# Fixed start addresses for the operands of the weight products in a one-layer HGRN2 + ConvFFN kernel

## The chip, the cores and the metric

The kernel runs on one core of a Trainium2 chip. Its time is the device time of one execution in microseconds (us). The median of three executions before the change is 1764.19 us (1764.08 to 1764.83).

## The reference

One layer of a hybrid backbone with `D_MODEL` 2048 works on 256 latent tokens `x` and 256 context tokens `ctx`, all in float32. Cut to what matters here:

```python
mods = silu(c) @ ada_w + ada_b                     # 2048 x 12288, shift/scale/gate rows
h_l, h_c = modulate(rms_norm(x) ...), modulate(rms_norm(ctx) ...)
q, f_fw, f_bw, v, g = split(h @ hgrn_w_in, 5)      # 2048 x 10240
o = bidirectional gated scan over q, f, v          # 16 heads of 128
y = (rms_norm(o) * silu(g)) @ hgrn_w_out           # 2048 x 2048
x1 = x + gate * rms_norm(y)
gate, up = split(modulate(rms_norm(x1) ...) @ ffn_w_in, 2)   # 2048 x 11264
out = x1 + gate2 * rms_norm((silu(conv3(gate)) * up) @ ffn_w_out)   # 5632 x 2048
```

Nearly all arithmetic is in the four products with `hgrn_w_in`, `hgrn_w_out`, `ffn_w_in` and `ffn_w_out`. Context tokens go through `hgrn_w_in` only.

## The kernel before

Every float32 operand of a weight product is split in two float32r parts, a high part (ScalarE's cast, L95) and the rest (VectorE's subtraction, L96). One product then becomes three matmuls, issued by `mm3`: high by high (L192), high by low (L193), low by high (L194). Below they are called the first, second and third matmul of a triple.

The weights come as a stream of 456 tiles (`Stream`), each 128 partitions by 1024 float32, 4096 bytes per partition. SyncE loads tile i to `w_raw`; `prep` splits it into `w_hi` and `w_lo`, three buffers each, two tiles ahead of its use. The stages, in order of the stream, are:

- Start (tiles 0 to 39): the first four heads' columns of `hgrn_w_in`, beside the shift and scale columns of `ada_w`. Both kinds of matmul below occur, with 256 and 512 columns.
- Loop (tiles 40 to 159): for each further pair of heads, `f` and `b` (weights stationary, 512 columns moving, `proj_ws`), `q` and `g` (weights stationary, 256 columns, `one_bank`) and `v` (tokens stationary, 256 weight columns moving, `proj_xs`). The scan of earlier heads runs beside it.
- Mixer's output product (tiles 160 to 191): tokens `zh`, `zl` stationary, 512 weight columns moving.
- FFN in (tiles 192 to 367): weights stationary, 256 columns of `h2h`, `h2l` moving. One tile gives 24 matmuls, eight triples. These are 176 tiles and 4224 matmuls.
- FFN out (tiles 368 to 455): tokens `ah`, `al` stationary, 512 weight columns moving, 12 matmuls per tile, 1056 in all.

A matmul's two operands lie in SBUF at byte addresses that are the same in every partition. `shifted` (L98 to L101) makes each `w_hi` and `w_lo` buffer 32 elements longer than the tile and lets tile i begin 16 * (i mod 8) bytes into it. A buffer thus takes 4224 bytes, 16.5 times 256, so that neighbouring buffers differ by 128 in their place modulo 256. In the built program the three `w_hi` buffers begin at 39424, 43648 and 47872, which is 0, 128 and 0 modulo 256, and the `w_lo` buffers at 52096, 56320 and 60544, which is 128, 0 and 128. Of one tile the high part and the low part are always 128 apart modulo 256. The other operands begin, modulo 256, at 0 (`h2h`, `h2l`), 224 (`hTh`, `hTl`, `ah`, `al`) and 160 (`zh`, `zl`). Slices within a tile step by 512 or 1024 bytes, which changes nothing modulo 256.

While one matmul streams its moving operand, TensorE loads the stationary operand of the next one. The text below calls *distance* the start address of that next stationary slice minus the start address of the moving slice that is streamed, modulo 256. For FFN in, with the moving operand on 0, the distance is the place of `w_hi` (during the first and third matmul, whose successors take `w_hi`) or of `w_lo` (during the second). With eight shifts and three buffers the same pairs of places come back after 24 tiles. Of FFN in, tile n (n from 0) is stream tile 192 + n and has the shift 16 * (n mod 8); tiles with n mod 8 = 4 have `w_hi` on 64 and `w_lo` on 192, or, in the middle buffer, `w_hi` on 192 and `w_lo` on 64.

Of the kernel before, what the change touches and what calls it, by code (L numbers as in the profile page):

```python
# [8 lines left out]
F32 = mybir.dt.float32  # L9
F32R = mybir.dt.float32r  # L10
# [7 lines left out]
P = 128  # L18
# [17 lines left out]
def tile_hgrn2_convffn_layer(  # L36
# [13 lines left out]
    wpool = ctx.enter_context(tc.tile_pool(name="wpool", bufs=3))  # L50
# [3 lines left out]
    ps_mi = ctx.enter_context(tc.tile_pool(name="ps_mi", bufs=1, space=PSUM))  # L54
    ps_o = ctx.enter_context(tc.tile_pool(name="ps_o", bufs=1, space=PSUM))

    def bank(pool, name):
        return pool.tile([P, 512], F32, name=name)

# [35 lines left out]
        S.copy(out=hi, in_=src)  # L95
        V.tensor_tensor(out=lo, in0=src, in1=hi.bitcast(F32), op=ALU.subtract)  # L96

    def shifted(pool, a, w, name, i):  # L98

        t = pool.tile([P, a * w + 32], F32R, name=name)  # L100
        return t[:, 4 * i:4 * i + a * w].rearrange("p (a n) -> p a n", a=a)  # L101

    class Stream:


# [14 lines left out]
        def prep(self, pool=wpool):  # L120
            i = len(self.done)
            with tc.high_priority(offset=0 if i < n_start else 400):
                self.load(i + 1)
                _, a, w = self.specs[i]
                hi = shifted(pool, a, w, "w_hi", i % 8)
                lo = shifted(pool, a, w, "w_lo", i % 8)
                if i in self.fine:
                    for j in range(a):
                        split(hi[:, j], lo[:, j], self.raw[i][:, j])
                else:  # L130
                    split(hi, lo, self.raw[i])
            self.raw[i] = None
            self.done.append((hi, lo))
# [250 lines left out]
    def ada_load(j2):  # L384
        aws = []
        for r4 in range(4):
            aw = st.tile([P, 4, 2, 256], F32, name="aw", bufs=4)
            for s in range(2):
                nc.sync.dma_start(
                    out=aw[:, :, s, :],  # L390
                    in_=ada_w[r4 * 512:(r4 + 1) * 512, s * D + j2 * 256:s * D + (j2 + 1) * 256].rearrange(
                        "(a p) n -> p a n", p=P))
            aws.append(aw)
        return aws
# [111 lines left out]
    with tc.manual_schedule():  # L506
        nc.sync.dma_start(out=rowsS[0:16], in_=rows128(c[0]))
        nc.sync.dma_start(out=rowsS[16:32], in_=rows128(c_ctx))
        load_tokens(x, xt)
        nc.sync.dma_start(out=rowsB[0:96], in_=rows128(ada_b))  # L510
        nc.sync.dma_start(out=rows0[0:16], in_=rows128(n_mix_pre[0]))
        ws.load(1)
        aws0 = ada_load(0)
        ws.load(4)
        V.memset(ones32, 1.0)
        V.memset(one1, 1.0)
        V.memset(eps1, EPS)
        nc.gpsimd.memset(cst, 0.0)
        make_identity(nc, ident)
        silu_c()  # L520
        normed(0)
        ws.prep()
        column(colsB, rowsB, 96)
        column(cols0, rows0, 16)
        strip = bank(ps_o, "o")
        ada_rows(strip, aws0, 0)
        turned(0, 0, KT)
        for r4 in range(1, 4):
            ada_rows(strip, aws0, r4)
        mod0 = ada_mod(0, strip)  # L530
        load_tokens(ctx_in, xt)
        for i in range(2):
            q4 = hpool.tile([P, 4, 512], F32R, name=f"hTh{i}")
            for k in range(4):
                hTh[4 * i + k] = q4[:, k]
        for k in range(2):
            hTl[k] = hpool.tile([P, 512], F32R, name=f"hTl{k}")
        modulated(0, mod0, (0,))
        ws.prep()
        ws.prep()  # L540
# [361 lines left out]
    yp = y_ctx.enter_context(tc.tile_pool(name="yp", bufs=1, side="right"))  # L902
    zh = [yp.tile([P, 2, T], F32R, name=f"zh{p}") for p in range(NP)]
    zl = [yp.tile([P, 2, T], F32R, name=f"zl{p}") for p in range(NP)]
    h_ctx, xin_ctx = ExitStack(), ExitStack()
    h2h, h2l, xin, hold = [], [], [], []

    def mixed():

        nonlocal h2  # L910
        with tc.high_priority(offset=200):
            split(zh[1], zl[1], z[1])
        for p in (*range(2, NP - 1), 0):
            split(zh[p], zl[p], z[p])
            for _ in range(MIXSTEP):
                next(mix, None)
            yield
        for _ in mix:
            pass
        split(zh[NP - 1], zl[NP - 1], z[NP - 1])  # L920
        yield
        yield
        zp_ctx.close()
        sp_ctx.close()
        h2 = h_ctx.enter_context(tc.tile_pool(name="h2", bufs=1))
        for k in range(KT // 2):
            h2h.append(h2.tile([P, 2, T], F32R, name=f"h2h{k}"))
            h2l.append(h2.tile([P, 2, T], F32R, name=f"h2l{k}"))

        xinp = xin_ctx.enter_context(tc.tile_pool(name="xinp", bufs=1))  # L930
        hold.append(xin_ctx.enter_context(tc.tile_pool(name="hold", bufs=MORE)))
        for i in range(4):
            xin.append(xinp.tile([P, D // 2], F32, name=f"xin{i}"))
            nc.sync.dma_start(out=xin[i], in_=x[i // 2 * P:(i // 2 + 1) * P, i % 2 * 1024:(i % 2 + 1) * 1024])

    h2 = None
# [172 lines left out]
```

## Time and profile before

| | us |
|---|---|
| median of three executions | 1764.19 |
| profiled execution, its own time | 1765.91 |
| span of the profiled execution, first to last instruction | 1764.1 |
| TensorE busy (matmul rows) | 1718.5 |
| VectorE busy | 1158.9 |
| ScalarE busy | 778.1 |

Matmuls overlap in the pipeline: a 256-column matmul is listed with some 281 ns, but the next one starts some 118 ns after it. The number that counts for the time is therefore not a row's duration but the distance in time from one matmul's start to the next one's, called the *pace* below. It is read from the timeline, whose first column is the start: start of the first matmul of the next tile minus start of the first matmul of this one, over the number of matmuls between.

### The profile page before, as it was taken

Reading aid. Unit: us, or ns where it says so; the run is one execution under the profiler, and the core shown is the slowest. Engines: PE = TensorE matmul, PEld = TensorE weight load, DVE = VectorE, ACT = ScalarE, POOL = GpSimd, SP = SyncE. Lnnn points to the kernel's source line nnn. Section 1 sums busy time; section 2 is a strip of 40 time slices with the busy share of each in tenths; the row PEclk is TensorE's granted clock in tenths of the full one; section 3 lists DMA queues with packets and bytes.
Section 4 is the critical chain, followed back from the end, with each engine's and each line's share of the span. In section 5 each row is a group of like instructions: output and inputs, shape, how many; then the busy total and the mean of one; then the engine's idle time right before and its main releaser. Section 6 shows DMA issues by size and latency. Waiting matters only on the chain.

```text
span 1764.1 us, 32106 instructions
## 1 busy us (share of the span) xinstructions
PE 1718.5 (97%) x13022; PEld 1530.1 (87%) x13022; DVE 1158.9 (66%) x1877; ACT 778.1 (44%) x1197; POOL 3.4 (0%) x13
## 2 busy tenths in 40 slices
PE   6999999999999999999999899999999999999998
PEld 4777788989889888988987699999999999888886
DVE  6777898855649775784667887565555565544444
ACT  4222264444545344443554644444444444443443
POOL 0000000000000000000000000000000000000000
PEclk9999999999999999999999899999999999999999
DMA  9887656643337764774368587566566565655554
GB/s 347 291 306 229 210 167 216 218 141 108 97 96 221 259 204 142 252 227 135 111 235 286 172 290 247 182 190 183 183 185 188 183 191 182 201 196 192 196 188 147
DMA packets 274646, 352.57 MB, mean 200 GB/s; under 512 B 12954, under 2 KB 197675, under 8 KB 273987
## 3 DMA queue, kind: packets, MB, share of 16 engines
q1 hardware_dynamic: 274499, 350.53, 61.6%
q8 instruction: 102, 1.67, 0.4%
q14 instruction: 45, 0.37, 0.1%
HBM read 348.37 MB, written 2.11 MB: 199 GB/s over the span
## 4 chain that ended last, share of the span: by engine, by line
PE 76%; DMA 11%; DVE 8%; issue 2%; ACT 2%; SPq 0%; DVEq 0%; ACTq 0%
PE pj L192 24%; PE pj L194 23%; PE pj L193 23%; DMA ada_w<-in_ada_w_dram 10%; DVE ada_acc L346 3%; DVE w_lo L96 2%; PE o L398 2%; PE sc L713 1%; ACT w_hi L95 1%; PE mi L785 1%; DMA aw<-in_ada_w_dram 0%; DVE k L673 0%; DMA w_raw<-in_hgrn_w_in_dram 0%; PE mi L701 0%; PE o L804 0%
## 5 line engine op out<-in xcount | busy, mean ns | idle before, releaser
L96 DVE TENSOR_TENSOR w_lo<-w_raw,w_hi 128x1024 fp32r<-128x1024 f32 (+1 forms) x465 | 558.5, 1203 | 383.8 <-ACT w_hi L95 382.6
L95 ACT CAST w_hi<-w_raw 128x1024 fp32r<-128x1024 f32 (+1 forms) x465 | 478.6, 1032 | 728.7 <-PE pj L193 395.7
L194 PE MATMUL pj<-h2h,w_lo 128*128 128x256 f32 x1408 | 395.9, 281 | 2.5 <-DVE w_lo L96 2.5
L193 PE MATMUL pj<-h2l,w_hi 128*128 128x256 f32 x1408 | 396.4, 282 | 0.1
L192 PE MATMUL pj<-h2h,w_hi 128*128 128x256 f32 x1408 | 396.0, 281 | 0.2 <-ACT h2h L95 0.2
L192 PE MATMUL pj<-hTh,w_hi 128*128 128x256 f32 (+1 forms) x1040 | 354.0, 341 | 2.8 <-ACT hTh L95 1.6
L194 PE MATMUL pj<-hTh,w_lo 128*128 128x256 f32 (+1 forms) x1040 | 347.9, 335 | 2.9 <-DVE w_lo L96 2.8
L193 PE MATMUL pj<-hTl,w_hi 128*128 128x256 f32 (+1 forms) x1040 | 348.0, 335 | 0.0
L194 PEld LDWEIGHTS pj<-h2h,w_lo 128*128 128x128 f32 x1408 | 265.8, 189 | 3.1 <-DVE w_lo L96 3.0
L192 PEld LDWEIGHTS pj<-h2h,w_hi 128*128 128x128 f32 x1408 | 265.7, 189 | 1.2 <-issue 0.8
L193 PEld LDWEIGHTS pj<-h2l,w_hi 128*128 128x128 f32 x1408 | 265.7, 189 | 0.3 <-DVE h2l L96 0.3
L346 DVE SCALAR_TENSOR_TENSOR ada_acc<-ada_w,cst,ada_acc 128x512 f32<-128x512 f32 x240 | 179.8, 749 | 77.9 <-DMA ada_w<-in_ada_w_dram 75.5
L192 PEld LDWEIGHTS pj<-hTh,w_hi 128*128 128x128 f32 x1040 | 195.5, 188 | 32.3 <-issue 5.9
L194 PEld LDWEIGHTS pj<-hTh,w_lo 128*128 128x128 f32 x1040 | 195.5, 188 | 25.7 <-DVE w_lo L96 3.5
L193 PEld LDWEIGHTS pj<-hTl,w_hi 128*128 128x128 f32 x1040 | 196.0, 188 | 21.0 <-DVE hTl L96 0.2
L192 PE MATMUL pj<-w_hi,ah 128*128 128x512 f32 x352 | 138.8, 394 | 0.0
L194 PE MATMUL pj<-w_hi,al 128*128 128x512 f32 x352 | 138.5, 393 | 0.0
L193 PE MATMUL pj<-w_lo,ah 128*128 128x512 f32 x352 | 138.1, 392 | 0.0
L192 PE MATMUL pj<-w_hi,hTh 128*128 128x256 f32 (+1 forms) x448 | 135.9, 303 | 1.3 <-DVE stage L448 0.7
L194 PE MATMUL pj<-w_hi,hTl 128*128 128x256 f32 (+1 forms) x448 | 133.8, 299 | 0.0
L193 PE MATMUL pj<-w_lo,hTh 128*128 128x256 f32 (+1 forms) x448 | 133.5, 298 | 0.0
L192 PEld LDWEIGHTS pj<-w_hi,hTh 128*128 128x128 f32 x448 | 85.0, 190 | 6.2 <-DVE stage L448 1.8
(224 smaller groups left out, 1778.8 us busy)
## 6 DMA issues: line engine op xcount, KB each, us to landing
w_raw<-in_ffn_w_in_dram SPq DMA_DIRECT2D x176, 512.0 KB, 4.5
w_raw<-in_hgrn_w_in_dram SPq DMA_DIRECT2D x160, 512.0 KB, 4.3
ada_w<-in_ada_w_dram SPq DMA_DIRECT2D x256, 256.0 KB, 3.9
w_raw<-in_ffn_w_out_dram SPq DMA_DIRECT2D x88, 512.0 KB, 3.7
aw<-in_ada_w_dram SPq DMA_DIRECT2D x64, 512.0 KB, 8.0
w_raw<-in_hgrn_w_out_dram SPq DMA_DIRECT2D x32, 512.0 KB, 5.6
hTh<-in_x_dram SPq DMA_DIRECT2D x2, 1024.0 KB, 7.1
hTh<-in_ctx_dram SPq DMA_DIRECT2D x2, 1024.0 KB, 11.8
```

Of the source, the lines that this page charges most:

```text
L95: S.copy(out=hi, in_=src)
L96: V.tensor_tensor(out=lo, in0=src, in1=hi.bitcast(F32), op=ALU.subtract)
L192: PE.matmul(out=o, lhsT=lh, rhs=rh, start=first, stop=False, skip_group_check=True)
L193: PE.matmul(out=o, lhsT=lh, rhs=rl, start=False, stop=False, skip_group_check=True)
L194: PE.matmul(out=o, lhsT=ll, rhs=rh, start=False, stop=last, skip_group_check=True)
L346: V.scalar_tensor_tensor(out=acc, in0=aw, scalar=cst[:, r, 0:1], in1=acc, op0=ALU.mult, op1=ALU.add)
L398: PE.matmul(out=strip[32 * a:32 * (a + 1), :], lhsT=cst[:, r4 * 4 + a, :], rhs=aws[r4][:, a].rearrange("p s n -> p (s n)"), start=(r4 == 0 ...
L713: PE.matmul(out=o[32 * b:32 * b + 32, 32 * i:32 * i + 32], lhsT=flat(lhs[b % 2])[:, s0:s0 + 32], rhs=flat(rhs[b % 2])[:, t0:t0 + 32], star ...
L785: PE.matmul(out=sps[:, cs], lhsT=kT[:, d, h, ct], rhs=v[:, 2 + ct, h * P:(h + 1) * P], start=(ct == 0), stop=(ct == 1))
```

## The change

The buffers of the split weights lose the 32 extra elements and the shift: they are 4096 bytes, and a 64-byte spacer ahead of them puts every one on 64 modulo 256. Spacers in other pools put the other operands of weight products on 0 modulo 256. In the built program after the change `w_hi` and `w_lo` begin on 64 modulo 256 in all buffers, the two pairs of held tiles of the output product included, and `hTh`, `hTl`, `zh`, `zl`, `h2h`, `h2l`, `ah` and `al` on 0. The one exception is `z0`, first tokens of the mixer's output product, on 64; it takes part in 12 matmuls. Pools of the scan (`f`, `stage`, `q`, `v`, `tmp` and the like) move from 0 to 64.

So the distance becomes 64 in all products with stationary weights and 0 - 64 = 192 in all with moving weights, for each matmul of a triple alike. The order of instructions on every engine, with the semaphores that they wait for, is row for row the same in both programs, but for line numbers and buffer numbers.

```diff
--- before.py
+++ after.py
@@ -54,6 +54,16 @@
     ps_mi = ctx.enter_context(tc.tile_pool(name="ps_mi", bufs=1, space=PSUM))
     ps_o = ctx.enter_context(tc.tile_pool(name="ps_o", bufs=1, space=PSUM))
 
+    def spacer(pool, nbytes):
+
+        pool.tile([P, nbytes // 4], F32, name="spacer", bufs=1)
+
+
+
+    SHIFT = 64
+    edge = ctx.enter_context(tc.tile_pool(name="edge", bufs=1, side="right"))
+    spacer(edge, 224)
+
     def bank(pool, name):
         return pool.tile([P, 512], F32, name=name)
 
@@ -95,11 +105,6 @@
         S.copy(out=hi, in_=src)
         V.tensor_tensor(out=lo, in0=src, in1=hi.bitcast(F32), op=ALU.subtract)
 
-    def shifted(pool, a, w, name, i):
-
-        t = pool.tile([P, a * w + 32], F32R, name=name)
-        return t[:, 4 * i:4 * i + a * w].rearrange("p (a n) -> p a n", a=a)
-
     class Stream:
 
 
@@ -122,8 +127,8 @@
             with tc.high_priority(offset=0 if i < n_start else 400):
                 self.load(i + 1)
                 _, a, w = self.specs[i]
-                hi = shifted(pool, a, w, "w_hi", i % 8)
-                lo = shifted(pool, a, w, "w_lo", i % 8)
+                hi = pool.tile([P, a, w], F32R, name="w_hi")
+                lo = pool.tile([P, a, w], F32R, name="w_lo")
                 if i in self.fine:
                     for j in range(a):
                         split(hi[:, j], lo[:, j], self.raw[i][:, j])
@@ -510,6 +515,7 @@
         nc.sync.dma_start(out=rowsB[0:96], in_=rows128(ada_b))
         nc.sync.dma_start(out=rows0[0:16], in_=rows128(n_mix_pre[0]))
         ws.load(1)
+        spacer(wpool, SHIFT)
         aws0 = ada_load(0)
         ws.load(4)
         V.memset(ones32, 1.0)
@@ -902,6 +908,7 @@
     yp = y_ctx.enter_context(tc.tile_pool(name="yp", bufs=1, side="right"))
     zh = [yp.tile([P, 2, T], F32R, name=f"zh{p}") for p in range(NP)]
     zl = [yp.tile([P, 2, T], F32R, name=f"zl{p}") for p in range(NP)]
+    spacer(yp, 192)
     h_ctx, xin_ctx = ExitStack(), ExitStack()
     h2h, h2l, xin, hold = [], [], [], []
 
@@ -923,12 +930,14 @@
         zp_ctx.close()
         sp_ctx.close()
         h2 = h_ctx.enter_context(tc.tile_pool(name="h2", bufs=1))
+        spacer(h2, 256 - SHIFT)
         for k in range(KT // 2):
             h2h.append(h2.tile([P, 2, T], F32R, name=f"h2h{k}"))
             h2l.append(h2.tile([P, 2, T], F32R, name=f"h2l{k}"))
 
         xinp = xin_ctx.enter_context(tc.tile_pool(name="xinp", bufs=1))
         hold.append(xin_ctx.enter_context(tc.tile_pool(name="hold", bufs=MORE)))
+        spacer(hold[0], SHIFT)
         for i in range(4):
             xin.append(xinp.tile([P, D // 2], F32, name=f"xin{i}"))
             nc.sync.dma_start(out=xin[i], in_=x[i // 2 * P:(i // 2 + 1) * P, i % 2 * 1024:(i % 2 + 1) * 1024])
```

## Rows read from the trace of the kernel before

**Rows 1.** The page: busy time with share and instructions, granted clock in 40 slices.

```profile
PE 1718.5 (97%) x13022; PEld 1530.1 (87%) x13022; DVE 1158.9 (66%) x1877; ACT 778.1 (44%) x1197; POOL 3.4 (0%) x13
...
PEclk9999999999999999999999899999999999999999
```

**Rows 2.** Stretches by stage: length, busy time of PE, PEld, DVE, ACT, POOL, clock, DMA.

```profile
320.00:890.00 570.00, 564.96 (x5267) 507.44 (x5266) 388.76 (x776) 263.02 (x506) 0.99 (x2) 1.00 0.53 168
...
1250.00:1512.00 262.00, 262.00 (x2221) 262.00 (x2219) 156.27 (x176) 121.14 (x141) 0.00 (x0) 1.00 0.61 187
1512.00:1764.00 252.00, 244.74 (x1061) 198.47 (x1059) 118.07 (x109) 96.42 (x105) 0.00 (x0) 0.99 0.56 186
```

**Rows 3.** Matmul groups by form: busy us, mean ns of one, idle before.

```profile
L193 PE MATMUL pj<-h2l,w_hi 128*128 128x256 f32 x1408 | 396.4, 282 | 0.1
...
L192 PE MATMUL pj<-hTh,w_hi 128*128 128x512 f32 x496 | 198.7, 401 | 0.0
...
L193 PE MATMUL pj<-hTl,w_hi 128*128 128x256 f32 x544 | 152.4, 281 | 0.0
...
L192 PE MATMUL pj<-w_hi,ah 128*128 128x512 f32 x352 | 138.8, 394 | 0.0
...
L193 PE MATMUL pj<-w_lo,hTh 128*128 128x256 f32 x384 | 108.3, 282 | 0.0
```

**Rows 4.** The longest wait within the weight products: us in total, times, longest.

```profile
PE pj L194 <- DVE w_lo L96: 5.3, 4, 2.6
```

**Rows 5.** Timeline, FFN in: first matmuls of tiles 100, 101, 108, 109 and 124.

```profile
1296.94 0.28 PE L192 MATMUL pj<-h2h,w_hi 128*128 128x256 f32 x1
...
1299.67 0.28 PE L192 MATMUL pj<-h2h,w_hi 128*128 128x256 f32 x1
...
1319.58 0.28 PE L192 MATMUL pj<-h2h,w_hi 128*128 128x256 f32 x1
...
1322.43 0.28 PE L192 MATMUL pj<-h2h,w_hi 128*128 128x256 f32 x1
...
1365.00 0.28 PE L192 MATMUL pj<-h2h,w_hi 128*128 128x256 f32 x1
```

**Rows 6.** Timeline inside tile 100: a matmul and the weight load beside it.

```profile
1297.96 0.28 PE L192 MATMUL pj<-h2h,w_hi 128*128 128x256 f32 x1
1297.97 0.19 PEld L193 LDWEIGHTS pj<-h2l,w_hi 128*128 128x128 f32 x1
```

**Rows 7.** Timeline, loop: two tiles of 24 matmuls with stationary weights, 256 columns.

```profile
525.73 0.28 PE L192 MATMUL pj<-hTh,w_hi 128*128 128x256 f32 x1
...
528.46 0.28 PE L192 MATMUL pj<-hTh,w_hi 128*128 128x256 f32 x1
...
531.28 0.27 PE L825 MATMUL mi<-ident,tmp 128*128 128x128 f32 x1
```

**Rows 8.** Timeline, loop: 45 matmuls of a tile with moving weights, 256 columns.

```profile
859.10 0.28 PE L192 MATMUL pj<-w_hi,hTh 128*128 128x256 f32 x1
...
864.28 0.28 PE L194 MATMUL pj<-w_hi,hTl 128*128 128x256 f32 x1
```

**Rows 9.** Timeline, loop: two tiles of 24 matmuls with stationary weights, 512 columns.

```profile
822.02 0.40 PE L192 MATMUL pj<-hTh,w_hi 128*128 128x512 f32 x1
...
827.59 0.40 PE L192 MATMUL pj<-hTh,w_hi 128*128 128x512 f32 x1
...
832.92 0.39 PE L194 MATMUL pj<-hTh,w_lo 128*128 128x512 f32 x1
```

**Rows 10.** Timeline, FFN out: first matmuls of three tiles of 12 matmuls each.

```profile
1540.07 0.39 PE L192 MATMUL pj<-w_hi,ah 128*128 128x512 f32 x1
...
1562.24 0.39 PE L192 MATMUL pj<-w_hi,ah 128*128 128x512 f32 x1
...
1565.02 0.39 PE L192 MATMUL pj<-w_hi,ah 128*128 128x512 f32 x1
...
1606.69 0.39 PE L192 MATMUL pj<-w_hi,ah 128*128 128x512 f32 x1
```

## The prediction

> **What bounds the kernel now.** I read the page first. TensorE is busy 97% of the span, and its granted clock stands at nine tenths or more in 39 of 40 slices [rows 1], so at the upper level, 2.4 GHz, nearly throughout. The stretches by stage say the same for each part: in the loop PE is busy 564.96 of 570.00 us, in the second half of FFN in 262.00 of 262.00, in FFN out 244.74 of 252.00 with the tail behind the last matmul, while VectorE has at most 68% of such a stretch (388.76 of 570.00) and the transfers a share of at most 0.61 [rows 2]. Within the weight products the longest wait of a matmul on another engine sums to 5.3 us [rows 4]. The end is therefore set by the number of matmuls and their pace, and the count is unchanged: 3 x (1408 + 544 + 384) = 7008 matmuls with 256 columns and some 3120 with 512 [rows 3].
>
> So I looked for what moves the pace, in the timeline. FFN in is the cleanest place, since there the same pairs of places come back every 24 tiles. From the first matmul of tile 100 to that of tile 124 pass 1365.00 - 1296.94 = 68.06 us for 576 matmuls, a mean pace of 118.2 ns [rows 5]. Tile 100 itself, with `w_hi` on 64 and `w_lo` on 192, takes 2.73 us for 24, 113.7 ns. Tile 108, with the two places exchanged, takes 2.85 us, 118.8 ns [rows 5]. Both run at the full clock, with the same work on either side. What they differ in is where the parts of the weights lie, and the load of the next stationary slice runs beside the matmul: it is issued at 1297.97, 0.01 us after the matmul that it accompanies, which began at 1297.96 [rows 6]. The distance between the two streams therefore decides some 4.5 ns per matmul, or 4%.
>
> The Trainium skill says the contrary ("SBUF — State Buffer", section "Who interferes with whom"): TensorE has two independent read ports, one for the moving operand and one for the weight load, and never waits on anyone. By that rule the addresses are without effect and the change is worth nothing. The two tiles just named speak against it; it stays as a rival below, with a small chance.
>
> **The change part by part.** The instructions and their order do not change, nor do the waits. What changes is the distance, to 64 for stationary weights and 192 for moving ones.
>
> (a) FFN in, 4224 matmuls. After the change every matmul has the distance 64. Before, tiles such as tile 100 have 64 in the first and third matmul and 192 in the second. That all three be at 64 is not shown by any tile. But in tile 100 a third matmul is followed by a first, so two matmuls in a row at 64 do occur there without loss. I take tile 100's pace, 113.6, within the rounding of its 2.73 us: (118.2 - 113.6) x 4224 = 19.4 us less. The ends: 113.3 if the loss at each change of tile goes too (20.7 us), and tile 108's pace, 118.8 (2.5 us more).
>
> (b) Loop, `q` and `g`, 6 x 2 x 96 = 1152 matmuls with stationary weights and 256 columns. A tile with distance 64 takes 528.46 - 525.73 = 2.73 us, the one behind it 2.82 us, 113.7 and 117.5 ns [rows 7]. The mean duration of the form is 281 ns, as in FFN in (282) [rows 3], so I put its mean pace at 118 too: 4.3 x 1152 = 5.0 us less. The other 480 of this form are in the start, where transfers and the adaLN work share the limit; full price 2.1 us, of which I take 1.0.
>
> (c) Loop, `v` with 256 moving weight columns, 1152 matmuls, distance 192 throughout. The nearest row of the same form is a tile whose distances are 64 and 192: 45 matmuls start within 864.28 - 859.10 = 5.18 us, 117.7 ns [rows 8], no gain. But there the moving operand itself jumps by 128 between high and low part, which it does not in FFN in and will not after the change. Ends: 4.2 x 1152 = 4.9 us less if it behaves as FFN in, 1 us more (0.8 ns each, as tile 108 is over the mean). The two nearest rows contradict each other and I take the middle, 2.5 us less.
>
> (d) All matmuls with 512 columns, about 3120: 1488 with stationary weights, the rest with moving ones. In the loop a tile with distances 64 and 192 takes 5.57 us for 24, 232.1 ns, and the next one, with other distances, 5.33 us for 23, 231.7 ns [rows 9]. In FFN out a tile at 192 and 64 takes 1565.02 - 1562.24 = 2.78 us for 12, 231.7 ns; the mean over 24 tiles is (1606.69 - 1540.07) / 288 = 231.3 ns [rows 10]. The good distance of the short matmuls does nothing here, and I take 0. Ends: the 4.6 ns of (a) on each, 14.4 us less, and twice tile 108's excess of 0.7 ns, since they are twice as long, 1.4 x 3120 = 4.4 us more.
>
> (e) The smaller buffers and the moved pools change no row count, so they are put at nothing. What covers them is TensorE's own stream. When FFN in runs 4% faster, VectorE goes from 156.27 / 262 = 60% to 62%, and the transfers' share from 0.61 to 0.64 [rows 2]: neither becomes late.
>
> Sum: 19.4 + 5.0 + 1.0 + 2.5 = 27.9 us less. The profiled execution took 1765.91 us (span 1764.1), so 1738.0; the median of the runs is 1.7 us below that execution, which gives 1736.3, about 1736.
>
> As to a floor, the Trainium skill ("TensorE: Matmul & The Clock Gate", section "Back-to-back issue gap") puts the isolated gap of a warm matmul at its columns over 2.4 GHz plus 2.5 ns, an estimate of 109 ns for 256 columns. The best tile here stands at 113.7 [rows 5], so by the page some 4 ns would be left; no row of this trace reaches it and nothing above uses it.
>
> **The rivals.**
> - Everything follows the distance, the long matmuls too: 19.4 + 5.0 + 1.0 + 4.9 + 14.4 = 44.7 us less, 1719. For it: after the change no operand jumps any more, which no 512-column tile shows. Against it: in rows 9 the moving operand does not jump either, and the pace is 232. Chance 0.12.
> - The gain is partial: the second matmul, at 64 where tile 100 had 192, does not keep up, or (b) stays as it is, and about half of the sum remains, 1750. Chance 0.10.
> - The wrong state is held. Tile 108 has the same two distances as tile 100, on other matmuls of the triple, and runs slow for its whole length [rows 5]. With one distance everywhere, nothing ever moves the streams out of whichever state they fall into, where before the next tile did. Its place is FFN in, and it decides if the second matmul's distance of 64 is the bad one. Price: 0.7 ns x 7008 = 4.9 us, and 4.4 us for the long matmuls from (d): 9.3 us more, 1773. Chance 0.10.
> - No effect: the tiles differ by something else that the places only mark, and the mean stays, 1764. That is also the page's rule on the ports. Against it: tiles of the same shift in the other buffer differ (100 and 108), with the same lines and loads. Chance 0.06.
>
> **How the numbers follow.** The forecast has the remaining 0.62, with its own range of 1725 to 1746 from the ends of (a) to (c). Adding the first two rivals (0.12 and 0.10) gives a range of 1716 to 1752 that leaves out the slow and the null case, 0.16. A change under 0.2%, 3.5 us, cannot be told from none in this kernel's runs. Faster: 0.62 + 0.12 + 0.10 = 0.84; same: 0.06; slower: 0.10.
>
> **What would show it.** In FFN in the first matmuls of tiles that follow each other should stand 2.72 to 2.73 us apart, every tile alike, where now it is 2.84 on the mean; the mean duration of its three forms should fall from 282 to about 277 ns. Loop tiles of `q` and `g` should take 2.73 us. The 512-column forms should keep 394 to 401 ns, and the `v` form should tell by its duration (282 now) which end of (c) holds. VectorE's and ScalarE's busy times should stay within 1%. The forecast is wrong if FFN in keeps a pace over 116 ns, or if TensorE's waits within the weight products grow from 5 us to over 10.

## The result and the profile after

The changed kernel takes 1743.60 us (median of four executions, 1739.16 to 1748.88) where the kernel before took 1764.51 beside it (four, 1764.08 to 1768.79). The ratio is 0.9878 with the interval 0.9846 to 0.9910, so 20.9 us were gained. Run again beside the experiments, it stood at 0.9883 (0.9849 to 0.9917). The profiled execution of the changed kernel is the longest of its four: 1748.88 us, span 1747.1. That is 17.0 us under the span of the profile before.

The page first, TensorE's busy time and its granted clock in 40 slices, which answer to [rows 1]. TensorE is busy 28.8 us less and still 97% of its span, with nine tenths or more of the full clock in every slice:

```profile
PE 1689.7 (97%) x13022; PEld 1501.7 (86%) x13022; DVE 1159.0 (66%) x1877; ACT 777.5 (45%) x1197; POOL 3.4 (0%) x13
...
PEclk9999999999999999999999999999999999999999
```

The stretch of the loop (length, busy time of PE, PEld, DVE, ACT, POOL, granted clock, DMA share, GB/s), cut at about the same work as in [rows 2]:

```profile
320.00:885.00 565.00, 552.55 (x5196) 493.47 (x5195) 383.85 (x767) 256.58 (x497) 0.99 (x2) 1.00 0.53 167
```

VectorE and ScalarE did the same work in the same time (1159.0 and 777.5 us in all). In the loop TensorE is now idle 565.00 - 552.55 = 12.45 us, where it was idle 5.04 before. A second profile of the same kernel has 9.65 there.

The matmul groups by form (busy us, mean ns of one, idle before) answer to [rows 3]. FFN in's group fell from 282 to 276 ns. Of the 512-column groups the one with stationary weights stayed at 401, and the first matmul of FFN out fell from 394 to 388. The last two groups are the first and third matmul of `v`, at 287 and 283 before:

```profile
L198 PE MATMUL pj<-h2l,w_hi 128*128 128x256 f32 x1408 | 389.1, 276 | 0.0
...
L197 PE MATMUL pj<-hTh,w_hi 128*128 128x512 f32 x496 | 198.8, 401 | 0.0
...
L197 PE MATMUL pj<-w_hi,ah 128*128 128x512 f32 x352 | 136.6, 388 | 0.0
...
L197 PE MATMUL pj<-w_hi,hTh 128*128 128x256 f32 x384 | 108.8, 283 | 0.0
...
L199 PE MATMUL pj<-w_hi,hTl 128*128 128x256 f32 x384 | 106.9, 278 | 0.0
```

The timeline of the changed kernel (start, duration, engine, line, operation) gives the paces and answers to [rows 5] and [rows 7 to 10]:

```profile
539.67 0.28 PE L197 MATMUL pj<-w_hi,hTh 128*128 128x256 f32 x1
...
545.21 0.28 PE L199 MATMUL pj<-w_hi,hTl 128*128 128x256 f32 x1
...
735.58 0.28 PE L197 MATMUL pj<-hTh,w_hi 128*128 128x256 f32 x1
...
738.30 0.28 PE L197 MATMUL pj<-hTh,w_hi 128*128 128x256 f32 x1
...
827.77 0.39 PE L197 MATMUL pj<-hTh,w_hi 128*128 128x512 f32 x1
...
833.14 0.40 PE L199 MATMUL pj<-hTh,w_lo 128*128 128x512 f32 x1
...
849.86 0.28 PE L197 MATMUL pj<-w_hi,hTh 128*128 128x256 f32 x1
...
855.30 0.28 PE L197 MATMUL pj<-w_hi,hTh 128*128 128x256 f32 x1
...
1291.04 0.28 PE L197 MATMUL pj<-h2h,w_hi 128*128 128x256 f32 x1
...
1293.76 0.28 PE L197 MATMUL pj<-h2h,w_hi 128*128 128x256 f32 x1
...
1312.80 0.28 PE L197 MATMUL pj<-h2h,w_hi 128*128 128x256 f32 x1
...
1315.52 0.28 PE L197 MATMUL pj<-h2h,w_hi 128*128 128x256 f32 x1
...
1356.32 0.28 PE L197 MATMUL pj<-h2h,w_hi 128*128 128x256 f32 x1
...
1520.42 0.39 PE L197 MATMUL pj<-w_hi,ah 128*128 128x512 f32 x1
...
1586.34 0.39 PE L197 MATMUL pj<-w_hi,ah 128*128 128x512 f32 x1
```

- FFN in, tiles 100, 101, 108, 109 and 124: every tile takes 2.72 us, and 1356.32 - 1291.04 = 65.28 us for 576 matmuls is 113.3 ns each. In [rows 5] it was 118.2, and tile 108, which took 2.85 us there, takes 2.72 like the others.
- Loop, `q` and `g`: 738.30 - 735.58 = 2.72 us for 24, 113.3 ns; in [rows 7] one tile of two took 2.82.
- Loop, `v`: one tile takes 855.30 - 849.86 = 5.44 us for 48, 113.3 ns; another has 47 matmul starts in 545.21 - 539.67 = 5.54 us, 117.9 ns. Both have the distance 192 in every matmul. In [rows 8] it was 117.7.
- Loop, 512 columns with stationary weights: 833.14 - 827.77 = 5.37 us for 23, 233.5 ns. [rows 9] had 231.7 for the same piece.
- FFN out: (1586.34 - 1520.42) / 288 = 228.9 ns, where [rows 10] had 231.3.

The waits (us in total, times, longest) answer to [rows 4]. TensorE's longest group of waits within the weight products went from 5.3 to 10.1 us; with its neighbour on L198 the pair went from 9.8 to 15.0. First the changed kernel, then the neighbour's line of the kernel before:

```profile
DVE ada_acc L351 <- DMA ada_w<-in_ada_w_dram: 80.2, 72, 3.7
...
PE pj L199 <- DVE w_lo L106: 10.1, 6, 4.2
...
PE pj L198 <- DVE w_lo L106: 4.9, 4, 2.3
...
PE mi L707 <- DVE ctmp L698: 1.7, 2, 1.0
PE sc L719 <- ACT scB L734: 1.6, 1, 1.6
...
PE pj L193 <- DVE w_lo L96: 4.5, 4, 1.5
```

The two lines with `mi` and `sc` are matmuls of the scan that wait for VectorE and ScalarE. All such waits of the scan sum to 9.0 us, where they were 4.3 before. In the second profile of the changed kernel the growth is smaller, 10.7 us for the `w_lo` pair and 6.8 for the scan:

```profile
PE pj L199 <- DVE w_lo L106: 7.3, 5, 3.6
...
PE pj L198 <- DVE w_lo L106: 3.4, 3, 1.9
```

The table collects the mean pace, in ns, of each kind of product over the whole trace: all pairs of neighbouring matmuls of a triple stream between which nothing else stands and nothing waits. d is the distance. "Given back" is all other time between the first and the last weight product beyond that of the profile before: waits, other matmuls, and time at the lower clock.

| kernel | FFN in | loop and start, stationary 256 | loop, moving 256 | loop and start, stationary 512 | FFN out | given back, us |
|---|---|---|---|---|---|---|
| before, d rotates | 118.1 | 117.9 | 118.0 | 232.3 | 231.2 | 0 |
| after, d 64 stationary, 192 moving | 113.4 | 114.2 | 116.4 | 233.3 | 228.9 | 11.9 |
| the same, second profile | 113.4 | 114.1 | 116.1 | 233.3 | 228.9 | 5.8 |
| d 0 everywhere | 120.0 | 119.8 | 119.9 | 227.4 | 226.7 | |
| d 192 stationary, 64 moving | 117.7 | 116.7 | 114.6 | 229.7 | 233.3 | |
| weights alone moved | 117.5 | 118.1 | 119.9 | 234.2 | 233.3 | |
| the same program, second profile | 113.6 | 118.1 | 119.9 | 234.1 | 233.3 | |
| other operands alone moved | 118.1 | 118.0 | 118.1 | 232.4 | 231.5 | -7.2 |

From the first two lines the change's account follows: FFN in 4224 x 4.74 = 20.0 us, stationary 256 1632 x 3.72 = 6.1, moving 256 1152 x 1.57 = 1.8, FFN out 1056 x 2.27 = 2.4, the other 564 matmuls with 512 moving columns 1.0, and minus 1.5 for 1488 x 1.01. That is 29.8 us from the pace. 11.9 were given back and the first weight product began 0.8 us later, which leaves 17.1, where the two profiles differ by 17.0. The last row has the paces of the kernel before, and yet 7.2 us less of all other time than the profile that is the zero of the column. What was given back is therefore known to some 7 us only.

### The profile page after: what moved, and what is told of

Read it like the earlier page. It is cut to its first block, busy times and chain, and to the rows that moved or that the text cites. A ratio compares the mean times of both kernels' runs of the same rounds, so it can differ in the third digit from the quotient of the medians.

```text
span 1747.1 us, 32106 instructions
## 1 busy us (share of the span) xinstructions
PE 1689.7 (97%) x13022; PEld 1501.7 (86%) x13022; DVE 1159.0 (66%) x1877; ACT 777.5 (45%) x1197; POOL 3.4 (0%) x13
## 3 DMA queue, kind: packets, MB, share of 16 engines
HBM read 348.37 MB, written 2.11 MB: 201 GB/s over the span
## 4 chain that ended last, share of the span: by engine, by line
PE 74%; DMA 12%; DVE 9%; issue 3%; ACT 1%; SPq 1%; DVEq 0%; ACTq 0%
PE pj L197 23%; PE pj L198 23%; PE pj L199 23%; DMA ada_w<-in_ada_w_dram 10%; DVE w_lo L106 3%; DVE ada_acc L351 2%; PE o L403 1%; DMA w_raw<-in_hgrn_w_in_dram 1%; DVE k L679 1%; PE sc L719 1%; ACT w_hi L105 1%; PE mi L791 1%; DMA aw<-in_ada_w_dram 1%; DMA hTh<-in_x_dram 0%; DVE QA L679 0%
## 5 line engine op out<-in xcount | busy, mean ns | idle before, releaser
L199 PE MATMUL pj<-h2h,w_lo 128*128 128x256 f32 x1408 | 389.5, 277 | 4.8 <-DVE w_lo L106 4.7
L197 PE MATMUL pj<-h2h,w_hi 128*128 128x256 f32 x1408 | 389.2, 276 | 0.0
L198 PE MATMUL pj<-h2l,w_hi 128*128 128x256 f32 x1408 | 389.1, 276 | 0.0
L198 PE MATMUL pj<-hTl,w_hi 128*128 128x256 f32 (+1 forms) x1040 | 348.2, 335 | 0.0
L198 PEld LDWEIGHTS pj<-h2l,w_hi 128*128 128x128 f32 x1408 | 264.4, 188 | 0.2 <-DVE h2l L106 0.2
L351 DVE SCALAR_TENSOR_TENSOR ada_acc<-ada_w,cst,ada_acc 128x512 f32<-128x512 f32 x240 | 179.8, 749 | 82.4 <-DMA ada_w<-in_ada_w_dram 80.2
L198 PEld LDWEIGHTS pj<-hTl,w_hi 128*128 128x128 f32 x1040 | 197.1, 190 | 21.4 <-DVE hTl L106 0.2
L198 PE MATMUL pj<-w_lo,ah 128*128 128x512 f32 x352 | 138.0, 392 | 0.0
L198 PE MATMUL pj<-w_lo,hTh 128*128 128x256 f32 (+1 forms) x448 | 132.3, 295 | 0.0
```

Source lines behind the costliest of these rows:

```text
L197: PE.matmul(out=o, lhsT=lh, rhs=rh, start=first, stop=False, skip_group_check=True)
L198: PE.matmul(out=o, lhsT=lh, rhs=rl, start=False, stop=False, skip_group_check=True)
L199: PE.matmul(out=o, lhsT=ll, rhs=rh, start=False, stop=last, skip_group_check=True)
L351: V.scalar_tensor_tensor(out=acc, in0=aw, scalar=cst[:, r, 0:1], in1=acc, op0=ALU.mult, op1=ALU.add)
```

## The experiments

Three questions were open: whether it is the distance that sets the pace, or some other property of the places; whether one distance gives one pace, or two that can hold themselves; and whether what was given back are waits behind VectorE's adaLN steps.

**Distance 0 everywhere.**

```diff
-    SHIFT = 64
+    SHIFT = 0
-        spacer(wpool, SHIFT)
-        spacer(hold[0], SHIFT)
```

> All buffers as long and as constant as in the changed kernel, but the weights on 0 modulo 256 like the other operands: distance 0 everywhere instead of 64 and 192. Theory A (the distance of the two read streams sets the pace, and 64 is the good one): FFN in falls back to the 119.0 ns per matmul of tiles with distance 0 before, loop tiles with stationary weights to about 118.9, so some 5.5 x 4224 + 4.7 x 1152 = 29 us over the changed kernel, about 1770 us. Rival B (what helps is that every tile begins on a whole multiple of 64 bytes and never moves): pace 113.4 as in the changed kernel, 1740 to 1749 us.

Measured: 1762.71 us (10 executions, 1759.67 to 1765.99), ratio 0.9986 (0.9976 to 0.9996), 7 us under theory A's 1770. FFN in lost its gain as that theory has it; what it missed are the long matmuls. Equal places for all tiles are thus not what gains; the value of the distance is. From the timeline, first matmuls of tiles 100 and 124 of FFN in:

```profile
1294.21 0.28 PE L197 MATMUL pj<-h2h,w_hi 128*128 128x256 f32 x1
...
1363.34 0.28 PE L197 MATMUL pj<-h2h,w_hi 128*128 128x256 f32 x1
```

69.13 us for 576 is 120.0 ns, the worst pace of 256 columns in the study, and at the same distance the 512-column products have their best, 226.7 to 228.1. The two nearly cancel: 4224 + 1632 + 1152 short matmuls at about 1.9 ns more against some 3110 long ones at about 4.6 less.

**Distances exchanged, 192 stationary and 64 moving.**

```diff
-    SHIFT = 64
+    SHIFT = 192
```

> Weights on 192 modulo 256: distance 192 for stationary weights, 64 for moving ones, the changed kernel's two distances exchanged. Theory A with a period of 128: the same as the changed kernel, FFN in 113.4 to 114 ns, 1740 to 1749 us. Rival (two states, the slow one held, as in tile 108 before, where the first and third matmul had 192): FFN in 119.1 ns throughout, about 1770 us.

Measured: 1761.86 us (1753.46 to 1764.19), ratio 0.9977 (0.9960 to 0.9994). The kinds exchange their paces with their distances: stationary 256 goes from 114.2 to 116.7 and moving 256 from 116.4 to 114.6, stationary 512 from 233.3 to 229.7 and FFN out from 228.9 to 233.3. So the distance decides the mean, not which operand is the weight. Theory A's period of 128 fell, and FFN in at 192 goes at 117.7. By tile these means are mixtures. At 64 and at 192 alike a tile of 256 columns goes at about 113.3 or at 117.8, and the distance sets how often: of 68 tiles with stationary weights 57 are at the short pace at 64 and 16 at 192, of the 24 tiles of `v` 18 at 64 and 7 at 192. The long matmuls with stationary weights have two paces at 192 as well, 54 of 62 tiles near 229 and 8 at 233.3, while at 64 all 62 stand at 233.3. FFN in had 174 of 176 tiles at the long pace here. That is one profile, and the runs with the weights alone moved show below how far two profiles of one program can lie apart.

**Weights alone moved, and the other operands alone.** The first leaves the other operands where they were (FFN in still has the distance 64, with the changed kernel's addresses modulo 256), the second keeps the rotating weights.

```diff
-    edge = ctx.enter_context(tc.tile_pool(name="edge", bufs=1, side="right"))
-    spacer(edge, 224)
-    spacer(yp, 192)
```

```diff
+    edge = ctx.enter_context(tc.tile_pool(name="edge", bufs=1, side="right"))
+    spacer(edge, 224)
+    spacer(yp, 192)
```

The first block is the edit of the changed kernel, the second that of the kernel before, without the definition of `spacer`.

> One part of the change alone: weights on 64 modulo 256, the others left where they were (hTh, hTl, ah, al on 224, zh, zl on 160, h2h, h2l on 0). FFN in has distance 64 as after the change, the loop 96 (stationary weights) and 160 (moving weights). Theory A: FFN in 113.4 ns; loop, stationary weights 256 columns 118.2, moving weights 118; about 20 us less than before, 1745 us, or some 1750 us with waits as in the changed kernel. Rival B (constant weights on multiples of 64 bytes are enough): loop 114 ns as after the change.

> The other part alone: hTh, hTl, ah, al, zh, zl on 0 modulo 256, the weights rotating as before. Distances are spread over all multiples of 16 as before. Theory A: no change of pace, FFN in 118.1 ns, loop 117.9, 512-column forms within 1 ns of before; 1764 us. Rival (misaligned moving operands cost by themselves): loop and FFN out faster by 2 ns or more per matmul, 1755 us or less.

Measured: weights alone 1759.63 us (10 executions, 1750.88 to 1772.10), ratio 0.9975 (0.9946 to 1.0004); others alone 1766.60 (1760.43 to 1771.02), ratio 1.0002 (0.9985 to 1.0019). Neither half is worth the change. The second half alone alters no pace. The surprise is in the first: FFN in, with the distance of the changed kernel, went at 117.5 ns. Its timeline, first matmuls of tiles 11 and 12, 14 and 15, 25 and 175:

```profile
1043.18 0.28 PE L195 MATMUL pj<-h2h,w_hi 128*128 128x256 f32 x1
...
1046.01 0.28 PE L195 MATMUL pj<-h2h,w_hi 128*128 128x256 f32 x1
...
1051.63 0.28 PE L195 MATMUL pj<-h2h,w_hi 128*128 128x256 f32 x1
...
1054.35 0.28 PE L195 MATMUL pj<-h2h,w_hi 128*128 128x256 f32 x1
...
1086.48 0.28 PE L195 MATMUL pj<-h2h,w_hi 128*128 128x256 f32 x1
...
1511.67 0.28 PE L195 MATMUL pj<-h2h,w_hi 128*128 128x256 f32 x1
```

Tile 11 takes 2.83 us, tile 14 takes 2.72, and from tile 25 to 175 pass 425.19 us for 3600 matmuls, 118.1 ns. By tile, 12 of 176 go at 113.3 and 164 at 117.8, and none stays near the middle. The short pace begins in tile 12 at a break of 0.17 us between two matmul starts (1046.12 to 1046.29), where 0.12 is usual, and ends in tile 24 at one of 0.37 (1083.42 to 1083.79). The distance alone does not decide.

**Low parts of the weights on 192, high parts on 64.**

```diff
+            self.apart = []
...
+                if pool not in self.apart:
+                    self.apart.append(pool)
+                    pool.tile([P, 32], F32, name="between", bufs=1)
                 lo = pool.tile([P, a, w], F32R, name="w_lo")
-        spacer(h2, 256 - SHIFT)
+        spacer(h2, 256 - SHIFT - 128)
```

> The changed kernel, but w_lo on 192 modulo 256 (128 behind w_hi, as it was in tile 100 before), by one 128-byte spacer between the two sets of buffers. Distances are 64, 192, 64 in a triple with stationary weights. Theory A2 (with one distance there are two states, 113.3 and 117.8 ns, and which one is held is chance; the alternation 64, 192, 64 draws the stream into the fast one, as all 15 such tiles before were fast): FFN in 113.4 to 113.7 ns in every tile, no run above 1752 us; moving weights 256 columns back to 118 ns, since the moving operand jumps by 128 again. Rival (the alternation does nothing, the state is chance here too): tiles of 117.8 ns held over long stretches, single runs near 1760 us.

Measured: 1741.07 us (1740.63 to 1747.45), ratio 0.9875 (0.9851 to 0.9898). FFN in goes at 113.4 with the distances 64, 192, 64 of tile 100 in [rows 5], so the second matmul's distance is free there. Of the 68 tiles with stationary weights of 256 columns none is at 117.8, the longest mean being 116.2, where the changed kernel has 8 to 16 at the long pace in its profiles. That is what theory A2 says of the alternation; FFN in does not tell, since the changed kernel held the short pace there too. `v` goes at 117.8, the pace of [rows 8], in all 24 tiles. Its moving operand jumps by 128 again, but its distances are also 192, 64, 192, those of tile 108 in [rows 5], which was as slow (118.8) without a jump. Which of the two costs in `v` is not shown.

**The changed kernel again, and the distances by form.** The second gives each kind of product the distance that the runs above favoured, as far as one place per operand allows: 192 for stationary weights in the loop, 64 for `v` and FFN in, 0 for the output product and FFN out.

```diff
-    spacer(edge, 224)
+    spacer(edge, 96)
-    spacer(yp, 192)
+    spacer(yp, 256)
+    spacer(ap, 64)
```

> The changed kernel once more, for the spread of its runs. Theory A2 (held state by chance): FFN in of 4224 matmuls is either at 113.3 or at 117.8 ns over most of its length, so runs fall between 1740 and 1759 us and some are in the upper half, as those of the weights-only kernel did with the same distance in FFN in (1751 to 1772). Rival (the state follows from the addresses and what runs beside them, and the changed kernel is always in the fast one): all runs 1739 to 1749 us.

> Each form gets the distance at which it was fastest so far, by moving tokens and activations, the weights staying on 64: hTh, hTl on 128 (distance 192 for stationary weights, 64 for moving ones: 229.0 ns for 512 columns against 233.3 after the change, 114.6 for moving 256 columns against 116.4, 116.7 for stationary 256 against 114.2), zh, zl, ah, al on 64 (distance 0: 227.4 and 226.7 ns against 229.2 and 228.9), h2h, h2l on 0 as in the changed kernel. Theory A: loop 4.2 x 1488 + 1.8 x 1152 - 2.5 x 1632 = 4.2 us less, output products 1.8 x 372 + 2.2 x 1056 = 3.0 us less, 1736 us where the changed kernel has 1743. Rival (waits on VectorE eat the loop's part, as they did in the changed kernel): 3 us less, 1740 us.

Measured: the changed kernel 1742.35 us (1738.86 to 1752.18), ratio 0.9883 (0.9849 to 0.9917), with one execution above the 1749 of the rival and FFN in at the short pace in the profile; by form 1739.48 (1735.73 to 1745.50), ratio 0.9865 (0.9833 to 0.9896). By form FFN out goes at 226.7, stationary 512 at 230.0 and `v` at 114.0, while stationary 256 rises to 117.4. Counted as above against the second profile of the changed kernel that is 4.2 us less; the medians differ by 2.9 and the intervals overlap, so it is the best version by its median alone, and 1736 was expected.

**Without the adaLN weight loads beside the loop, changed kernel and kernel before.** Three tiles of `ada_w`, loaded once, are used again in place of the later loads, so in these two kernels part of the result is not computed from its own weights.

```diff
+    held = []
-                aw = pool.tile([P, 512], F32, name="ada_w", bufs=3)
-                nc.sync.dma_start(out=aw, in_=ada_w[r * P:(r + 1) * P, part * D + b * 512:part * D + (b + 1) * 512])
+                aw = pool.tile([P, 512], F32, name="ada_w", bufs=3) if part == 5 or len(held) < 3 else held[r % 3]
+                if part == 5 or len(held) < 3:
+                    nc.sync.dma_start(out=aw, in_=ada_w[r * P:(r + 1) * P, part * D + b * 512:part * D + (b + 1) * 512])
+                    if part != 5:
+                        held.append(aw)
```

> The changed kernel with three ada_w tiles loaded once and reused for the adaLN parts that run beside the loop (the other loads of these parts are left out, so those gates are not the reference's). Theory W (the loop's gain was eaten by VectorE: its in-order queue holds w_lo behind an adaLN step that waits for its transfer): VectorE waits no more for ada_w in the loop (47 us before), TensorE's waits for w_lo fall from 15 us to under 8, and the time falls by 5 to 10 us, to about 1735. Rival (these waits are noise between runs): no change beyond 3 us.

> The kernel before, with the adaLN weight loads beside the loop left out: three tiles loaded first are used again, so that part of the result is not computed from its own weights. It is the counterpart of the changed kernel without these loads (1731.8 us). Theory W (the changed kernel gives back some 10 us of its pace gain to waits behind these loads, which hardly touched the kernel before): the time falls only by what TensorE idled in the loop of the kernel before, 3 to 6 us, to 1758 to 1761, so that the two kernels without loads differ by 26 to 29 us, the gain by pace alone, where with the loads they differ by 21 to 22. Rival (the loads cost both kernels the same, and the pace gain is really only 21 us): the time falls by the 10 us that the changed kernel fell by, to 1753 to 1754, and the difference stays 21 to 22. The paces of the weight products stay those of the kernel before in both (118.1 ns in FFN in, 231.2 in FFN out).

Measured: the changed kernel without the loads 1731.83 us (1726.89 to 1734.55), ratio 0.9811 (0.9787 to 0.9834); the kernel before without them 1755.98 (1751.30 to 1758.27), ratio 0.9951 (0.9936 to 0.9966). The first fell by 10.5 us and the second by 8.5. The waits of the changed kernel without the loads (us, times, longest):

```profile
DVE ada_acc L356 <- DMA ada_w<-in_ada_w_dram: 22.4, 20, 2.9
...
PE pj L198 <- DVE w_lo L106: 4.2, 3, 1.8
```

And of the kernel before without them:

```profile
DVE ada_acc L351 <- DMA ada_w<-in_ada_w_dram: 21.7, 19, 2.8
...
PE pj L193 <- DVE w_lo L96: 3.0, 3, 1.3
```

VectorE's wait for these loads falls to 22 us in both, from 75.5 before and 80.2 after, and the two kernels then differ by 24.1 us where with the loads they differ by 21 to 22. So theory W, as it was put, falls: the loads cost the kernel before nearly as much. The 2.0 us by which the two falls differ are inside the noise, since the interval of either ratio is 5 to 8 us wide. So no share of what was given back is shown to come from these loads. The loss is there without them too: between these two profiles the pace gives 30.0 us and the spans differ by 24.0. Part of it are, in the weight products behind the start, gaps of over 1 us (10.8 against 8.1 us in sum), in the output product and the first tiles of FFN in. The clock does not tell the two apart: between the first and the last weight product the lower level was granted for 13.7 us in each. Why `w_lo` comes later was not taken apart further.

**The adaLN steps spread over more tiles, in the changed kernel and in the one by form.**

```diff
-ADA_RATE = 3
+ADA_RATE = 2.45
-        if p >= 3:
-            ahead[0] += ADA_RATE * tiles
+        ahead[0] += ADA_RATE * tiles
```

> The changed kernel with the adaLN steps spread over more tiles: from the third product of the loop on at a rate of 2.45, not from the fourth on at 3. Nothing is left out. Theory W: a step's load has 20% more time to arrive before VectorE stands at it, so VectorE's waits for these loads fall from 72 to 80 us to under 50, TensorE loses less in the loop, and the time falls from 1742 by 3 to 8 us, to 1734 to 1739. Rival (the loads are late because of the load traffic as a whole, or VectorE's wait only moves to the added tiles): VectorE waits as long as before, and the time stays 1740 to 1744. The paces by form stay as in the changed kernel (FFN in 113.4 ns).

> The kernel with the distances by form (1739.5 us) with the adaLN steps spread over more tiles, as in the run beside it. Theory W: it falls by as much as that one, to 1731 to 1736. Rival: it stays at 1738 to 1741. Paces by form as in the run without the spread: FFN in 113.4, FFN out 226.7 ns.

Measured: 1742.82 us (1741.07 to 1747.08), ratio 0.9882 (0.9847 to 0.9918), and by form 1741.92 (1738.17 to 1752.92), ratio 0.9884 (0.9842 to 0.9926). Neither gains. The waits of the first show why; VectorE stands fewer times (61, not 72) but longer each time, and TensorE loses as much as in the first profile of the changed kernel:

```profile
DVE ada_acc L351 <- DMA ada_w<-in_ada_w_dram: 75.3, 61, 3.9
...
PE pj L199 <- DVE w_lo L106: 9.9, 5, 4.5
```

So the rate of the steps is not what makes the loads late, and the rival holds. The changed kernel's addresses held the long pace here for a while: behind a stop of 2.11 us, at 1050.29, tiles 15 to 21 of FFN in went at 117.8. In the profile by form with the spread, the first 15 tiles of FFN in went at 117.8 and nearly all others at 113.3.

**Weights alone, once more**, the same program as above for a second profile.

> The kernel with only the weights moved, once more, for the state of FFN in, whose addresses are those of the changed kernel modulo 256. In its first profile FFN in went at 117.5 ns, where the changed kernel had 113.4 in two profiles. Theory S (two paces hold themselves at this distance, and which one is entered hangs on how the streams stand at the entry, so that it can differ between executions of one program): the mean of FFN in may be anywhere from 113.4 to 117.8, and tiles have one of these two paces with few between. Rival F (the pace is fixed by the addresses and by what goes before in the program): 117.5 within 0.3, and the same tiles (about the 12th to the 23rd) are the fast ones again. A third reading, in which the pace is set by the distance alone, expects 113.4 and has the first profile against it.

Measured: 1756.41 us (8 executions, 1749.01 to 1759.50), ratio 0.9950 (0.9929 to 0.9970); the profiled execution has a span of 1748.0, against 1768.5 in the first profile of this program. Its timeline in FFN in (first matmuls of tiles 11, 12, 14, 15, 25 and 175, and two matmuls that waited):

```profile
1037.37 0.28 PE L195 MATMUL pj<-h2h,w_hi 128*128 128x256 f32 x1
...
1040.09 0.28 PE L195 MATMUL pj<-h2h,w_hi 128*128 128x256 f32 x1
...
1041.01 0.39 PE L197 MATMUL pj<-h2h,w_lo 128*128 128x256 f32 x1 [0.53 <-DVE w_lo L104]
...
1046.53 0.28 PE L195 MATMUL pj<-h2h,w_hi 128*128 128x256 f32 x1
...
1049.36 0.28 PE L195 MATMUL pj<-h2h,w_hi 128*128 128x256 f32 x1
...
1073.58 0.39 PE L197 MATMUL pj<-h2h,w_lo 128*128 128x256 f32 x1 [1.69 <-DVE w_lo L104]
...
1082.02 0.28 PE L195 MATMUL pj<-h2h,w_hi 128*128 128x256 f32 x1
...
1491.22 0.28 PE L195 MATMUL pj<-h2h,w_hi 128*128 128x256 f32 x1
```

Now tile 11 takes 2.72 us and tile 14 takes 2.83, the reverse of the first profile, and from tile 25 to 175 pass 409.20 us, 113.7 ns. Of 176 tiles 166 go at 113.3 and 10 at 117.8. The program, its addresses and its order are the same, so theory S holds: two paces hold themselves at the distance 64. The lines also show where they change. The short pace ends at a wait of 0.53 us (1041.01) and comes back at one of 1.69 us (1073.58). In all eight profiles with this distance in FFN in (twice this program, four with the changed kernel's places, two by form) the pace of FFN in changes for good only where the stream is interrupted. Behind a last break in tile 24 the pace then found holds to the end, more than 400 us, through six matmuls of another kind that take 1.2 us in tile 80. FFN in's pace accounts for (117.5 - 113.6) x 4224 = 16.5 of the 20.5 us between the two spans.

## Why the prediction was right, and where its steps were not

The time came out in the range, 7.6 us above the forecast. The mechanism, pace by distance, was right; the sum lacks one loss, and 1.9 us of gain at the long matmuls, which it had put at nothing, hid a part of it by luck. What the prediction did not have is that the distance only makes one of two paces more frequent.

- **(a), FFN in: right.** 19.4 us predicted, 20.0 in the profile; the pace is 113.4, and the last losses at the change of tile went too, which was its better end. The choice of tile 100's pace as the pattern was sound.
- **(b), stationary 256: right.** 6.0 predicted with the start, 6.1 found. Tiles of 2.72 us came as foreseen. In the start the pace varies from tile to tile between 113.3 and 117.8.
- **(c), moving 256: right in size, by another way.** 2.5 predicted as the middle of two ends, 1.8 found. It is no middle: each tile goes at one end or the other, 7 of 24 at 113.3 and 17 at 117.8 in the first profile.
- **(d), 512 columns: mis-sized.** 0 predicted, 1.9 us gained. The step that [rows 9, 10] show no effect of the distance was wrong: with 64 the long matmul goes at 233.3, with 192 at 229 to 231, with 0 at 227 to 228. Those tiles mixed the distances, and their mean hid both: (2 x 233.3 + 229.7) / 3 is 232.1, the very pace of the loop's tile. That the optimum of the short matmul is the pessimum of the long one was not foreseen.
- **(e), nothing else becomes late: wrong.** This is the term that failed: 11.9 us were given back in the first profile and 5.8 in the second, where the prediction has 0. The busy shares of VectorE and ScalarE stayed as forecast, but a share does not say who stands behind whom. In the first profile TensorE's waits for `w_lo` grew by 5.2 us and those of the scan's matmuls by 4.7, and the line of [rows 4] went to 10.1, over the 10 us that the prediction named as a sign against it. That profile is of the longest of four executions. In the second, near the median, the line is at 7.3, the waits grew by 0.9 and 2.5, and the lower clock was granted for 27.3 us between the first and the last weight product, where it was 20.5 before and 17.1 in the first profile. So the loss is there in both, and its make-up differs from execution to execution.

Two readings inside the prediction do not come out of its rows. Tile 108 is 118.8 - 118.2 = 0.6 ns over the mean, where (c) has 0.8 and (d) and the rival of the wrong state have 0.7. And the ends of (a) to (c) do not give 1725 to 1746: the good ends sum to 32.7 us, 1731.5, and the bad end of (a) alone lies at 1758. Ends, prices and the range rest on these, the sum does not.

The loads of the adaLN steps are not shown to be the cause of what was given back, by the two kernels without them; the loss was seen and placed, not explained. One place of the first profile shows how such a loss comes about. The timeline of the changed kernel, VectorE and TensorE:

```profile
630.30 0.28 PE L198 MATMUL pj<-hTl,w_hi 128*128 128x256 f32 x1
...
632.82 0.75 DVE L351 SCALAR_TENSOR_TENSOR ada_acc<-ada_w,cst,ada_acc 128x512 f32<-128x512 f32 x1 [2.32 <-DMA ada_w<-in_ada_w_dram]
...
633.49 1.22 DVE L106 TENSOR_TENSOR w_lo<-w_raw,w_hi 128x1024 fp32r<-128x1024 f32 x1
...
634.76 0.52 PE L199 MATMUL pj<-hTh,w_lo 128*128 128x256 f32 x1 [4.19 <-DVE w_lo L106]
```

VectorE stands 2.32 us for an `ada_w` transfer before 632.82; the `w_lo` of the next weight tile is queued behind it on the same engine and starts at 633.49; TensorE, whose last matmul starts at 630.30, goes on at 634.76 after 4.19 us without work. The kernel before had such waits too, 4 with 2.6 us at the longest [rows 4]. That a faster stream leaves VectorE less of a lead, so that the same lateness costs more, is the likely reading; no run shows it by itself. This stop cost more than the wait. The stretches before and behind it (columns as above) show the granted clock:

```profile
628.00:630.00 2.00, 2.00 (x20) 2.00 (x19) 1.75 (x3) 1.66 (x2) 0.00 (x0) 1.00 0.88 288
636.00:638.00 2.00, 2.00 (x11) 2.00 (x11) 2.00 (x4) 0.00 (x0) 0.00 (x0) 0.50 0.89 284
```

Behind the stop TensorE goes at 0.50, the lower of its two levels, 1.2 GHz, and has 11 matmuls in 2 us where it has 20 at the upper.

- **The wrong state is held: a real mechanism, in other kernels.** The rival said that with one distance nothing moves the streams out of the pace they fall into. Just this is seen where the weights alone were moved, and 20.5 us lie between two profiles of that one program. Its condition was wrong: the second matmul's distance does not decide, since 64, 64, 64 holds either pace and 64, 192, 64 went at 113.4. In FFN in the changed kernel's two profiles came out of every stop with the short pace for good; with the adaLN steps spread, the same places came out of one with the long pace for seven tiles. Of the 24 `v` tiles 17 and 15 stand at the long pace in the changed kernel's two profiles. What decides which pace follows a stop stays open.
- **Everything follows the distance, 1719:** the long matmuls do follow it, but in the other direction at 64, where they are slower. **Partial, 1750:** the median is not there. **No effect:** refuted, with the ends 113.3 and 120.0 ns for the same work.

The Trainium skill ("SBUF — State Buffer", section "Who interferes with whom") has the moving operand and the weight load on independent read ports, and TensorE never waiting on anyone. The traces do not agree with addresses being without effect, as 4224 matmuls go at 120.0 ns with distance 0 and at 113.4 with 64; what in the chip makes the difference, no run shows. The Trainium skill's isolated gap ("TensorE: Matmul & The Clock Gate", section "Back-to-back issue gap") gives an estimate of 109 ns for 256 columns. No held pace here reaches it; the best is 113.3.

## What to carry to other kernels

Where TensorE streams one operand and loads the next stationary one at the same time, look at the start addresses of both modulo 256: for float32r and 256 columns a difference of 64 gave up to 5.5% over equal places (120.0 to 113.4 ns), and for 512 columns equal places were best. A pace that can hold itself in two ways has to be profiled more than once, and so has what a change gives back. When the engine that bounds gets faster, the lead of what feeds it, in order of its queue, is a likelier guide than its busy share; no run here tests that by itself.

## What the runs showed of the hardware that was not expected

- Two held paces at one distance, 113.3 and 117.8 ns for 256 columns, at 64 and at 192 alike. In FFN in one gives way to the other for good only at a break in the stream, as short as 0.17 us between two starts, and not at every break; kept for as long as 400 us, they differ by 19 us over FFN in.
- The distance changes which of the two is frequent (57 of 68 tiles at the short pace at 64, 16 of 68 at 192), and at 0 every tile stands between 118.6 and 120.1.
- The best distance turns round with the length of the moving operand: 256 columns 120.0 ns at 0 and 113.4 (or 117.8) at 64; 512 columns 226.7 at 0, 233.3 at 64, 228.9 (or 233.3) at 192.
- A stop of 4.19 us was followed by some 3.5 us at the lower clock (634.76 to about 638.3), in which 16 matmuls started some 215 ns apart, about 1.7 us more lost.
